# The first two gate tiles of a mixer kernel: weight units in other homes, the seventh product's weights and the third operand's sum made ahead, the third product in the second's bank

## The chip, the cores and the metric

The kernel runs on one core of a Trainium2 chip, as one launch. The metric is the device time of one execution in microseconds (us), the median of several runs. The core has five queues of instructions that run side by side and wait for one another by semaphores. In the profile they are PE (the matrix engine; PEld is its weight load), DVE (elementwise work), ACT (activations and copies), POOL (here mostly an issuer of DMAs) and SP (issues DMAs only).

## The reference

One layer of a backbone runs on 640 tokens: 512 of a denoising step and 128 of a context prefix. Width is 1024. After a norm and a modulation, `h` goes through an input projection into four mixers a, b, c, d (short convolution, HGRN2, neighbourhood attention, chunked gMLP), each 256 wide. They are joined by gates, and this is the part that the change touches:

```
g_a, g_b, g_c, g_d = split(sigmoid(h @ w_gate + b_gate), 4)
merged = (g_a * (y_a @ w_br_a) + g_b * (y_b @ w_br_b)
          + g_c * (y_c @ w_br_c) + g_d * (y_d @ w_br_d))
return merged @ w_o, ...
```

`w_gate` is 1024 x 4096 and each `w_br` is 256 x 1024. After it come `w_o`, a residual, a second norm and a feed-forward part with a convolution. Everything is float32.

## The kernel before

**Precision.** A float32 matrix product is done as three passes of a reduced type: each operand is split into a high half (a copy rounded by ACT) and a low half (the operand less its high half, on DVE), and high x high, high x low and low x high are summed. So each new operand or weight costs an ACT copy and a DVE subtraction before PE can use it.

**The gate stage.** The 16 pairs of gate tiles, in the order of `PAIRS`, go through `g_pair0` (pair 0) and `g_pair` (pairs 1 to 15, and a closing call). A pair is 2 x 2 blocks of outputs and of inputs and is done with seven products in place of eight (a Strassen scheme). `gprod(o, p, i, first)` is product i of the gate weights with operand `gx["x"][i]`: 4 blocks x 3 passes = 12 matmuls of 128 x 320. `bprod` is the same product of the branch weights with `y`: 3 matmuls. The sums of products run in PSUM banks: `first=True` begins a bank anew, `False` adds to what it holds. So products 1, 6 and 7 share one bank, with an ACT copy of the partial sum taken between them; in `g_pair0` before, products 5 and 3 share bank `b2`.

**Weights.** A pair has three weight units A, B, C of 128 x 2560 and a small one Z, made from raw weights: A and C are raw blocks, B two sums S, and Z one sum. `g_a`/`g_al`, `g_b`, `g_c` and `g_zh`/`g_zl` make the high and low halves. Product 1 and 2 read A, 5 and 6 B, 7 Z, 4 and 3 C. `gunit` gives a unit its home: unit k = 3p + i lives in one of three rotating `wp` buffers, or, every fourth, in the region "B", which the attention uses until its last matmuls. The raw weights come by SP into three rotating `rp` buffers or the region "G" (`gp_load`). The sums of pairs 0 and 1 are not made on DVE: `up_a23` has POOL add them up in DRAM (`gsum`) by DMAs long before, and pairs 0 and 1 only load them.

**Operands.** Products 1, 2, 4 and 3 read quadrants of `h`. Operands 6, 5 and 7 are differences, made and split by the generator `g_operands` (`place`) into the regions F, X1 and X0. Operand 3 of all pairs is replaced by a sum t3, which `g_operands` adds up and `g_pair0` splits (`g_split(3, ...)`). The memory of t3 then holds S (`gx["S"]`): in pair 1 a POOL DMA brings it (`g_s01`).

**What sets the order.** The generators (`attn`, `g_operands`, `up_a23`) are advanced by `tick`, which each product calls with its estimated time; a generator waits by polling a flag in `R`. Until `g_all` sets `fixed[0]`, a planner places the instructions of each engine by readiness, and by program order among those that are ready. From then on the calls through `ovec`, `oact`, `opool` and `omm` stay in program order on their engines: an instruction that waits holds up all that were written after it on its engine. SP's loads are left to the planner. All pinned calls go through one line, so line 150 in the profile stands for most of the gate stage; it is read by tile names (`w`, `B`, `S` weights; `m`, `g` banks; `ga`, `gb`, `y` gate sums; D holds operand 7's source and then t3 and S; G holds y's sums).

**Lines.** `g_operands` is at 1019 to 1080, `gp_load` and `gunit` at 1133 to 1154, `g_s01` to `g_zl` at 1167 to 1207, `g_pair0` at 1269 to 1327, `g_pair` at 1329 to 1412, the sums in DRAM at 1616 to 1624.

## Time and profile before

| | |
|---|---|
| median of 3 runs | 1005.3 us (1005.0 to 1007.15) |
| the profiled execution: its own time, its span | 1005.73 us, 1003.8 us |
| PE, PEld busy | 987.3 us (98%), 934.4 us (93%) |
| DVE, ACT, POOL busy | 864.7 us (86%), 592.6 us (59%), 195.5 us (19%) |
| DMA, mean over the span | 224 GB/s |
| mean granted PE clock | 0.995 |

A row of a timeline reads: start in us from the span's beginning, duration, engine, line, operation, output tile <- input tiles, shape, count; in square brackets, how long the engine had been idle before it and what released it. Rows of equal kind that follow one another are merged. A row of a table by stretches reads: the stretch, its length, then PE, PEld, DVE, ACT and POOL busy in us with their instruction counts, the granted PE clock (1.00 is full speed), the busy share of the DMA engines, and GB/s. A matmul's end is modelled: in a full-speed stream one starts every 0.147 us though each is shown as 0.31.

### The profile page before, as it was taken

What the parts mean: (1) busy time and instruction counts of PE and PEld (TensorE: products, weight loads), DVE (VectorE), ACT (ScalarE), POOL (GpSimd) and SP (SyncE); (2) the same over time, 40 slices, a digit from 0 to 9 for tenths busy, and PEclk for the clock granted to TensorE, in tenths of its full rate; (3) what the DMA queues carried; (4) which work ended last, traced back from release to release, by engine and by line L of the source; (5) the groups of instructions that cost most, each with busy time, mean ns of one, the idle gap of its engine ahead of it and who ended that gap; (6) DMA issues with size and microseconds to landing.
All of it is one profiled execution on the core that took longest, in us unless ns stands there. A gap on an engine that the chain in (4) does not pass through costs nothing.

```text
span 1003.8 us, 18999 instructions
## 1 busy us (share of the span) xinstructions
PE 987.3 (98%) x7437; PEld 934.4 (93%) x7437; DVE 864.7 (86%) x1413; ACT 592.6 (59%) x1034; POOL 195.5 (19%) x267
## 2 busy tenths in 40 slices
PE   8999999999979999999999999999999999999997
PEld 7899999999979999999998899999999999888886
DVE  6679899879878789898877778999999998999796
ACT  6652343445565655655655376777777777756672
POOL 1000022324023122243210021222222222100004
PEclk9999999999999999999999999999999999999999
DMA  9886349698169699999948775766666666976842
GB/s 354 333 292 246 113 149 257 175 283 241 54 222 252 179 261 315 222 313 269 260 123 351 280 283 173 226 154 173 174 166 168 176 170 192 347 261 217 300 131 105
DMA packets 75769, 224.92 MB, mean 224 GB/s; under 512 B 10432, under 2 KB 25312, under 8 KB 72992
## 3 DMA queue, kind: packets, MB, share of 16 engines
q1 hardware_dynamic: 44400, 149.25, 42.2%
q0 software_dynamic: 31280, 74.46, 31.6%
q8 instruction: 58, 0.95, 0.4%
q14 instruction: 31, 0.25, 0.1%
HBM read 182.64 MB, written 59.39 MB: 241 GB/s over the span
## 4 chain that ended last, share of the span: by engine, by line
PE 90%; DVE 5%; DMA 2%; issue 1%; POOL 1%; ACT 1%; SPq 0%; POOLq 0%; DVEq 0%; ACTq 0%
PE m L150 23%; PE g L1721 21%; PE g L374 11%; PE m L2184 8%; PE m L1721 5%; PE g L150 5%; PE m L1474 4%; PE g L2184 4%; PE g L955 2%; PE g L1474 1%; PE m L539 1%; PE m L1716 1%; DMA A<-in_w_ada_dram 1%; POOL hss L317 1%; PE m L955 1%
## 5 line engine op out<-in xcount | busy, mean ns | idle before, releaser
L374 PE MATMUL g<-XH,w 128*128 128x320 f32 x576 | 140.6, 318 | 0.0
L374 PEld LDWEIGHTS g<-XH,w 128*128 128x128 f32 x576 | 98.7, 188 | 2.4 <-issue 1.2
L150 PE MATMUL m<-XH,w 128*128 128x320 f32 x416 | 98.4, 311 | 1.7 <-DVE gb L150 1.7
L374 PE MATMUL g<-XL,w 128*128 128x320 f32 x288 | 89.0, 309 | 0.0
L150 PEld LDWEIGHTS m<-XH,w 128*128 128x128 f32 x416 | 70.8, 188 | 3.5 <-ACT ga L150 2.1
L150 PE MATMUL m<-XL,w 128*128 128x320 f32 x208 | 63.0, 310 | 0.0
L2184 PE MATMUL m<-w,XH 128*128 128x512 f32 x246 | 58.7, 390 | 0.0
L2184 PEld LDWEIGHTS m<-w,XH 128*128 128x128 f32 x246 | 46.1, 188 | 9.5
L374 PEld LDWEIGHTS g<-XL,w 128*128 128x128 f32 x288 | 54.2, 188 | 0.1
L150 DVE TENSOR_TENSOR w<-raw,w 128x640 fp32r<-128x640 f32 (+3 forms) x47 | 48.5, 1048 | 2.6 <-ACT w L150 2.6
L150 ACT ACTIVATE w<-raw 128x640 fp32r<-128x640 f32 (+3 forms) x53 | 48.5, 931 | 1.7 <-DMA raw<-in_w_in_dram 1.1
L150 POOL DMA_DIRECT2D wsum<-in_w_dn_dram x36 | 37.3, 1239 | 47.9 <-issue 31.4
L150 ACT ACTIVATE gb<-m 128x320 f32<-128x320 f32 x32 | 14.0, 437 | 49.0 <-PE m L150 49.0
L150 DVE SCALAR_TENSOR_TENSOR X<-MG,p2t,X 128x641 f32<-128x641 f32 x44 | 38.9, 884 | 1.0 <-ACT X L150 0.2
L150 DVE SCALAR_TENSOR_TENSOR X<-X,p2t,X 128x641 f32<-128x641 f32 x44 | 38.9, 884 | 0.9
L150 PEld LDWEIGHTS m<-XL,w 128*128 128x128 f32 x208 | 38.6, 188 | 0.6 <-issue 0.6
L1721 PE MATMUL g<-XL,w 128*128 128x320 f32 x240 | 38.6, 310 | 0.0
L1721 PE MATMUL g<-XL,C 128*128 128x320 f32 x240 | 38.3, 309 | 0.0
L1721 PEld LDWEIGHTS g<-XL,w 128*128 128x128 f32 x240 | 36.0, 188 | 0.6 <-ACT MG L150 0.3
L1721 PEld LDWEIGHTS g<-XL,C 128*128 128x128 f32 x240 | 36.0, 188 | 0.0
L150 PE MATMUL m<-X,S 128*128 128x320 f32 x192 | 32.3, 318 | 1.9 <-DVE S L150 1.9
L150 PE MATMUL m<-XH,B 128*128 128x320 f32 x128 | 31.9, 318 | 1.8 <-ACT m L150 1.8
(624 smaller groups left out, 2923.5 us busy)
## 6 DMA issues: line engine op xcount, KB each, us to landing
wsum<-in_w_dn_dram POOLq DMA_DIRECT2D x30, 512.0 KB, 11.6
raw<-in_w_gp_dram SPq DMA_DIRECT2D x23, 640.0 KB, 7.0
raw<-in_w_up_dram SPq DMA_DIRECT2D x28, 512.0 KB, 5.3
raw<-in_w_in_dram SPq DMA_DIRECT2D x19, 512.0 KB, 4.6
H<-in_w_adt_dram SPq DMA_DIRECT2D x19, 512.0 KB, 4.3
G<-in_w_up_dram SPq DMA_DIRECT2D x12, 512.0 KB, 5.1
raw<-wsum SPq DMA_DIRECT2D x12, 512.0 KB, 6.4
actx<-X POOLq DMA_DIRECT2D x22, 256.0 KB, 4.6
```

The costliest lines, as they stand in the source:

```text
L150: r = f(*args, **kw)
L317: pool.tensor_tensor(out, out, neghalf[:, 0:n], ALU.pow)
L374: mm(o, w[:, h, k0 + k, :], r(k)[:, s], start=(k == 0 and i == 0), stop=(k == kt - 1 and i == 2))
L539: mm(m[W * g:W * g + W, (i - s0) * W:(i - s0 + 1) * W], lhs, rhs, start=True, stop=True, tile_position=(64 * par, W * g))
L955: mm(o, x(kx)[:, ts], w[:, h, k, :], start=(kx == 0 and i == 0), stop=(kx == 7 and i == 2))
L1474: mm(m, mh[MHN[q]][:, hx, k % 2, t * P:(t + 1) * P], wo[q][:, hw, k % 2, :], start=(k == 0 and i == 0), stop=(k == 7 and i == 2))
L1716: mm(o, w[:, k, :], x[:, k, :], start=(first and not part and k == 0 and j == 0), stop=(part == 1 and k == 3), skip_group_check=True)
L1721: z = mm(o, w[:, k, :], x[:, k, :], start=(first and k == 0 and j == 0), stop=(k == 3 and j == 2), skip_group_check=True)
L2184: mm(ps, s[t // 4][:, hx, k, o:o + P], w[:, hw, k, c0:c1], start=first, stop=i == 2 and bi == len(batch) - 1 and k == len(ks) - 1, skip_gr ...
```

## The change

- `gunit`: the region "B" now takes the units with k mod 4 = 2 (was 3). Unit C of pair 0 lives there, unit A of pair 1 in a `wp` buffer, and so on in turn.
- `gsum` grows from two pairs to three: POOL makes the sums of pair 2 as well (18 DMAs in place of 12), and pair 2 loads its S by a POOL DMA and its third sum by SP, in place of three additions on DVE.
- `gp_load`: all loads go by SP. Pairs 0 and odd pairs use two `rp` buffers, other even pairs one and the region "G" (was the other way round). Pair 1's second block is no longer loaded by POOL from within pair 0; pair 2's load is issued inside pair 0.
- `g_operands`: unit B of pair 0 is cast as soon as the tile `ab0` is done, without waiting for `ab1`; then operands 6 and 5, t3, and both halves of Z. Unit C is cast after the attention's last part (`yc`), then operand 7.
- `g_pair0`: product 4 comes after products 1 and 2; t3's split and the load of S for pair 1 come between products 4 and 6; pair 1's unit A is cast before product 5; `gb` takes product 5 off right after it; product 3 begins bank `b3` (the second product's) anew, and is added to `gb` in an operation of its own. Units B, C and Z of pair 1 are no longer made here.
- `g_pair(1)`: units B, C, and the high half of Z are cast after the copy of product 1's branch part, and the low halves of Z and C after product 2 is issued. Pair 2's S load is issued behind them, and its second sum (`g_s23`) after product 5.

```diff
--- before.py
+++ after.py
@@ -1051,32 +1051,30 @@
         g_s23(0, r)
         while "ab0" not in R:
             yield 0.5
-        lows = g_c(0, r)
-        low(*lows[0])
-        while "ab1" not in R:
-            yield 0.5
         b = gw[0, "B"] = gunit(0, 1)
-        for i in range(2):
-            oact(b[:, 0, 1 - i], s[1 - i], AF.Copy)
-        low(b[:, 1, 1], s[1], b[:, 0, 1])
+        for i in (1, 0):
+            oact(b[:, 0, i], s[i], AF.Copy)
+            low(b[:, 1, i], s[i], b[:, 0, i])
         while "scores" not in R:
             yield 0.5
         place(6, a11, "F")
+        yield 0.5
+        place(5, a22, "X1")
         R["gx3"] = True
-        yield 1
-        place(5, a22, "X1")
-        low(b[:, 1, 0], s[0], b[:, 0, 0])
         yield 0.5
         ovec.tensor_tensor(a22, a12, a11, ALU.add)
-        g_zh(0, r)
-        gx["t3"] = a22
         gx["S"] = a22.rearrange("p a t -> p (a t)").rearrange("p (i k c) -> p i k c", i=2, k=5)
         gx["Y"] = a11.rearrange("p a t -> p (a t)")
         y_load(0)
-        low(*lows[1])
+        g_zh(0, r)
+        g_zl(0, r)
+        gx["t3"] = a22
         while "yc" not in R:
             yield 0.5
+        lows = g_c(0, r)
+        low(*lows[0])
         place(7, a21, "X0")
+        low(*lows[1])
         gx["Y1"] = a21.rearrange("p a t -> p (a t)")
 
     def g_split(i, x):
@@ -1124,7 +1122,8 @@
     def gp_id(p_):
         return PAIRS[p_]
 
-    gsum = dram.tile([2, P, 3, 5, P], F32, name="gsum")
+    GSUM = 3
+    gsum = dram.tile([GSUM, P, 3, 5, P], F32, name="gsum")
 
     def gp_raw(p_, h):
         bi, n = gp_id(p_)
@@ -1134,22 +1133,18 @@
 
         r = [rp.tile([P, 2, 5, P], F32, tag="raw", name=nm("raw"))]
         nc.sync.dma_start(r[0], gp_raw(p_, 0))
-        if p_ != 1:
-            gp_load2(p_, r)
-        return r
-
-    def gp_load2(p_, r):
-        r.append(region("G", [P, 2, 5, P]) if p_ % 2 else rp.tile([P, 2, 5, P], F32, tag="raw", name=nm("raw")))
-        if p_ > 1:
+        r.append(rp.tile([P, 2, 5, P], F32, tag="raw", name=nm("raw")) if p_ % 2 or not p_
+                 else region("G", [P, 2, 5, P]))
+        if p_ >= GSUM:
             nc.sync.dma_start(r[1], gp_raw(p_, 1))
         else:
-            eng = opool if p_ else nc.sync
-            eng.dma_start(r[1][:, 0], gp_raw(p_, 1)[:, 0])
-            eng.dma_start(r[1][:, 1], gsum[p_][:, 2])
+            nc.sync.dma_start(r[1][:, 0], gp_raw(p_, 1)[:, 0])
+            nc.sync.dma_start(r[1][:, 1], gsum[p_][:, 2])
+        return r
 
     def gunit(p_, i):
         k = 3 * p_ + i
-        if k % 4 == 3:
+        if k % 4 == 2:
             return region("B", [P, 2, 2, 5, P], F32R)
         return wp.tile([P, 2, 2, 5, P], F32R, tag="w", name=nm("w"))
 
@@ -1167,8 +1162,8 @@
     def g_s01(p_, r):
 
         s = gw[p_, "S"] = [gx["S"][:, i] for i in range(2)]
-        if p_ == 1:
-            opool.dma_start(gx["S"], gsum[1][:, 0:2])
+        if p_ < GSUM:
+            opool.dma_start(gx["S"], gsum[p_][:, 0:2])
             return
         ovec.tensor_tensor(s[0], r[0][:, 0], r[1][:, 1], ALU.add)
         ovec.tensor_tensor(s[1], s[0], r[1][:, 0], ALU.add)
@@ -1176,7 +1171,7 @@
     def g_s23(p_, r):
         s = gw[p_, "S"]
         b21, (b22, b12) = r[0][:, 1], (r[1][:, 0], r[1][:, 1])
-        if p_ > 1:
+        if p_ >= GSUM:
             ovec.tensor_tensor(b12, b12, b22, ALU.add)
         ovec.tensor_tensor(b21, s[1], b21, ALU.add)
 
@@ -1279,51 +1274,43 @@
         oact(ga[:, 0:HC], b1, AF.Copy)
         bprod(p1_, 0, 1, True)
         oact(p3_, p1_, AF.Copy)
-        gprod(b4, 0, 4, True)
         gprod(b3, 0, 2, True)
         ovec.tensor_tensor(ga[:, 0:HC], b3, ga[:, 0:HC], ALU.add)
         g_sig(0, 0, ga[:, 0:HC], ga[:, 0:HC])
         bprod(p3_, 0, 2, False)
+        drain(lambda: "Y1" in gx)
+        gprod(b4, 0, 4, True)
+        g_split(3, gx["t3"])
+        g_s01(1, r[1])
         gprod(b1, 0, 6, False)
         oact(gb[:, 0:HC], b1, AF.Copy)
-        drain(lambda: "t3" in gx)
-        g_split(3, gx["t3"])
-        g_s01(1, r[1])
-        drain(lambda: "Y1" in gx)
+        g_a(1, r[1])
+        y_sums()
         gprod(b2, 0, 5, True)
-        g_zl(0, r[0])
-        g_a(1, r[1])
+        ovec.tensor_tensor(gb[:, 0:HC], b2, gb[:, 0:HC], ALU.subtract)
+        gx["C"] = region("MG1", [P, 2, 3, HC], F32R)
+        lows, x3 = y_split()
+        oact(x3[2], x3[1], AF.Copy)
         gprod(b1, 0, 7, False)
         oact(gb[:, HC:T], b1, AF.Copy)
-        y_sums()
+        for x in lows + [x3]:
+            low(*x)
         ovec.tensor_tensor(ga[:, HC:T], b4, gb[:, HC:T], ALU.add)
         g_sig(0, 0, ga[:, HC:T], ga[:, HC:T])
         ovec.tensor_tensor(gb[:, HC:T], b2, gb[:, HC:T], ALU.subtract)
-        gx["C"] = region("MG1", [P, 2, 3, HC], F32R)
-        lows, x3 = y_split()
-        oact(x3[2], x3[1], AF.Copy)
-        for x in lows + [x3]:
-            low(*x)
-        gp_load2(1, r[1])
+        r[2] = gp_load(2)
+        gprod(b3, 0, 3, True)
         g_al(1, r[1])
-        gprod(b2, 0, 3, False)
         y = gw[0, "y"] = gp.tile([P, T], F32, tag="gt", name=nm("y"))
         c2_ = gw[0, "b2"] = pm()[:, 0:HC]
         bprod(p1_, 0, 6, False)
         oact(y[:, 0:HC], p1_, AF.Copy)
+        ovec.tensor_tensor(gb[:, 0:HC], b3, gb[:, 0:HC], ALU.add)
         bprod(c2_, 0, 5, True)
-        ovec.tensor_tensor(gb[:, 0:HC], b2, gb[:, 0:HC], ALU.subtract)
         bprod(p1_, 0, 7, False)
         oact(y[:, HC:T], p1_, AF.Copy)
         ovec.tensor_tensor(y[:, HC:T], c2_, y[:, HC:T], ALU.subtract)
-        late = []
-        g_b(1, late)
         g_s23(1, r[1])
-        late += g_c(1, r[1])
-        r[2] = gp_load(2)
-        g_zh(1, r[1])
-        for x in late:
-            low(*x)
         gx["Y"] = gx["Y1"]
 
     def g_pair(p_, r):
@@ -1345,7 +1332,8 @@
         b1, b3 = pm()[:, 0:HC], pm()[:, 0:HC]
         ga = gw[p_, "gt", 0] = gp.tile([P, T], F32, tag="gt", name=nm("ga"))
         gb = gw[p_, "gt", 1] = gp.tile([P, T], F32, tag="gt", name=nm("gb"))
-        g_zl(p_, r[p_])
+        if q:
+            g_zl(p_, r[p_])
         gprod(b1, p_, 1, True)
         g_sig(q, 1, gw[q, "gt", 1], gw[q, "gt", 1])
         oact(b3, b1, AF.Copy)
@@ -1354,23 +1342,36 @@
         p1_, p3_ = ps[:, 1, 0:HC], ps[:, 0, 0:HC]
         bprod(p1_, p_, 1, True)
         oact(p3_, p1_, AF.Copy)
+        if not q:
+            g_b(p_)
+            late = g_c(p_, r[p_])
+            g_zh(p_, r[p_])
         g_merges(q)
         if nx:
             g_a(n, r[n])
+            if q:
+                g_s01(n, r[n])
+        gprod(b3, p_, 2, False)
+        if not q:
+            g_zl(p_, r[p_])
+            for x in late:
+                low(*x)
             g_s01(n, r[n])
-        gprod(b3, p_, 2, False)
         lows, x3 = y_split() if new else ([], None)
         g_sig(p_, 0, ga[:, 0:HC], b3)
         for x in lows:
             low(*x)
         if nx:
             g_al(n, r[n])
-            g_s23(n, r[n])
+            if q:
+                g_s23(n, r[n])
         gprod(b1, p_, 6, False)
         oact(gb[:, 0:HC], b1, AF.Copy)
         bprod(p3_, p_, 2, False)
         b2 = pm()[:, 0:HC]
         gprod(b2, p_, 5, True)
+        if not q:
+            g_s23(n, r[n])
         if nx and not new:
             g_b(n)
         gprod(b1, p_, 7, False)
@@ -1616,12 +1617,13 @@
         while "stc" not in R:
             yield 1
         for o, h, i, add in ((0, 0, 0, 0), (2, 1, 0, 0), (0, 1, 1, 1), (2, 1, 1, 1), (1, None, 0, 0), (1, 1, 0, 1)):
-            for p_ in range(2):
+            for p_ in range(GSUM):
                 bi, n = gp_id(p_)
                 g = gsum[p_][:, i] if h is None else gp_raw(p_, h)[:, i]
                 z = pool.dma_start(gsum[p_][:, o], g, accum_op=ALU.add) if add else pool.dma_start(gsum[p_][:, o], g)
                 tc.keep_in_program_order(z)
-                yield 0.7
+                if p_ != 1:
+                    yield 0.5
 
     def up_early():
         x = region("XH", [P, 5, 8, P])
```

## The prediction

> **What bounds the kernel now.** The page first: PE is busy 98% of the span, and the chain that ended last is PE for 90%. A table by stretches of 100 us has PE busy throughout in most of them (the row shown is after the gate stage).
>
> ```profile
> PE 90%; DVE 5%; DMA 2%; issue 1%; POOL 1%; ACT 1%; SPq 0%; POOLq 0%; DVEq 0%; ACTq 0%
> 700.00:800.00 100.00, 100.00 (x684) 100.00 (x683) 94.78 (x146) 71.72 (x124) 24.53 (x32) 1.00 0.63 169
> ```
>
> So a change on another engine counts only where PE waits. The grouped list of PE's waits has its three longest, one instruction each, in the gate stage. PE's timeline gives their places:
>
> ```profile
> 274.46 0.41 PE L150 MATMUL m<-XH,w 128*128 128x320 f32 x1
> ...
> 284.44 0.46 PE L150 MATMUL m<-X,S 128*128 128x320 f32 x2
> 286.80 3.00 PE L150 MATMUL m<-X,S 128*128 128x320 f32 x10 [1.90 <-DVE S L150]
> 291.53 0.39 PE L150 MATMUL m<-XH,w 128*128 128x320 f32 x1 [1.74 <-DVE gb L150]
> ...
> 297.75 0.60 PE L150 MATMUL g<-E,B 128*128 128x320 f32 x3
> 300.19 0.41 PE L150 MATMUL m<-XH,B 128*128 128x320 f32 x1 [1.84 <-ACT m L150]
> ...
> 305.34 0.60 PE L150 MATMUL g<-E,B 128*128 128x320 f32 x3
> 305.78 1.92 PE L150 MATMUL m<-X,w 128*128 128x320 f32 x12
> ...
> 314.00 0.46 PE L150 MATMUL m<-XH,w 128*128 128x320 f32 x2
> ```
>
> Three matmuls take 305.78 - 305.34 = 0.44 us, 0.1467 each; twelve take 1.76. Pair 0 starts at 274.46, pair 2 with the second matmul of the last row, at 314.15: 39.69 us for 204 matmuls (14 gate products of 12, 12 branch products of 3), which need 204 x 0.1467 = 29.92. Lost: 9.77 us. Product 7 starts at 284.44, so product 3 was due at 284.44 + 1.76 = 286.20 and starts at 291.53: 5.33. Pair 1's product 2 was due at 297.75 + 0.44 = 298.19 and starts at 300.19: 2.00. The 24 matmuls after it take 305.34 - 300.19 = 5.15 in place of 3.52: 1.63. The other 0.81 are small waits. The table by stretches shows why those matmuls are slow:
>
> ```profile
> 283.20:286.60 3.40, 1.70 (x12) 1.44 (x10) 2.09 (x2) 2.44 (x3) 0.29 (x1) 1.00 0.26 105
> 286.60:290.00 3.40, 3.00 (x10) 2.60 (x10) 2.02 (x5) 0.17 (x1) 0.24 (x1) 0.54 0.60 173
> 290.00:293.40 3.40, 1.87 (x13) 1.90 (x14) 2.34 (x5) 2.18 (x5) 0.00 (x0) 0.96 0.53 212
> 296.90:300.30 3.40, 1.56 (x11) 1.30 (x11) 3.40 (x5) 3.21 (x7) 2.29 (x4) 1.00 0.91 255
> 300.30:303.70 3.40, 3.40 (x14) 3.40 (x15) 3.27 (x6) 1.50 (x3) 2.47 (x4) 0.53 1.03 300
> ```
>
> Two stretches with PE busy for 1.70 and 1.56 of 3.40 us were each followed by one at half clock (0.54, 0.53); the one with 1.87 was not. I read from this that a stretch less than about half busy costs the next its clock. The Trainium skill, "TensorE: Matmul & The Clock Gate" (Part 1: The HAM clock gate), says that the clock falls to half after a whole idle window of some 3.4 us, and gives as rule to have no idle gap above that. By the rule the gaps here would cost no clock, and the sum below would be 1.63 + 1.37 = 3.0 us smaller; the trace decides against it.
>
> **Part 1, product 7 (wait for S).** These rows say why it waited:
>
> ```profile
> 273.76 1.37 ACT L150 ACTIVATE w<-s 128x640 fp32r<-128x640 f32 x2 [2.98 <-PE g L374]
> 275.19 1.26 ACT L676 ACTIVATE A<-MG 128x1280 fp32r<-128x1280 f32 x1
> 278.43 1.26 ACT L150 ACTIVATE X<-D 128x1280 fp32r<-128x1280 f32 x1
> 279.59 0.42 ACT L150 ACTIVATE ga<-m 128x320 f32<-128x320 f32 x1
> 279.90 0.43 ACT L150 ACTIVATE g<-g 128x320 f32<-128x320 f32 x1
> 284.51 1.49 DVE L150 TENSOR_TENSOR XL<-D,XH 128x1280 fp32r<-128x1280 f32 x1 [2.82 <-ACT XH L150]
> 285.92 0.82 DVE L150 TENSOR_TENSOR S<-raw,S 128x640 fp32r<-128x640 f32 x1
> 273.76 0.82 DVE L435 TENSOR_TENSOR MG<-g,MG 128x640 f32<-128x640 f32 x1 [2.66 <-PE g L374]
> ```
>
> Z's low half stood on DVE behind operand 3's (284.51), which waited for ACT. In the change t3's sum (1.49) and Z's halves (0.74, 0.82) are written while tile `ab1` runs, and the hole is there: before 273.76 DVE had been idle for 2.66 us and ACT for 2.98. It fits nearly (1.49 + 0.82 = 2.3), so I put the wait at nothing; if it does not fit, the last 0.8 to 2.3 us land on the chain of the next paragraph. Operand 3's split gets product 6, 5 and 7 (5.3 us) as cover. With the wait goes the half clock: the 10 matmuls took 3.00 in place of 1.63, 1.37 of the 5.33.
>
> **What is late next, (a).** Unit C of pair 0 now lives where the attention reads until 274.5, so its two copies (0.64 each from start to start) come after that, where B's were. On ACT from 274.57: attention's own copy 0.16, C 1.28, operand 7's high half 1.16, A<-MG 1.16, then `ga`'s copy 0.31, and the copy that the second branch product waits for ends 0.43 later, at 279.07; PE follows at 279.13. As product 4 no longer lies between, PE is there after 274.46 + 1.76 + 0.44 + 1.76 and 0.1 of small waits, at 278.53. Loss 0.60; nothing if the planner takes `ga` first, 2 more if Z's or t3's work lands here. C's low half needs 0.82 after 275.4 and product 4 comes at 279.6: covered.
>
> **Part 2, product 3 (wait for gb).** Its bank was the one that `gb` still had to be taken from. Bank `b3`'s last reader (`ga`, at 281.2 before) is long done, so this wait is gone: 5.33 - 2.07 - 1.37 = 1.89. The operation added on DVE (0.49) lies beside products 5 and 7. The next thing due is pair 1's unit A, at about 290.0 by PE. What DVE has to do before it:
>
> ```profile
> 292.05 1.23 DVE L150 TENSOR_TENSOR MG<-G,MG 128x640 fp32r<-128x640 f32 x2 [0.66 <-ACT MG L150]
> 293.19 0.49 DVE L150 TENSOR_TENSOR E<-G,E 128x320 fp32r<-128x320 f32 x1
> ```
>
> The lows of y (1.23 + 0.49), a `ga` and a `gb` operation (0.49 each) and A's low half (1.49, as XL above), 4.2 from 286.0, when y's sums are copied: 290.2, for the third matmul at 290.3. Just covered; each 0.5 that DVE is late would show.
>
> **Part 3, pair 1's product 2 (wait for m).** ACT made four casts and a sigmoid, from 295.65 on, in front of the copy at 299.72:
>
> ```profile
> 295.65 1.26 ACT L150 ACTIVATE w<-D 128x1280 fp32r<-128x1280 f32 x1
> 299.72 0.41 ACT L150 ACTIVATE m<-m 128x320 f32<-128x320 f32 x1
> 296.95 1.49 DVE L150 TENSOR_TENSOR w<-D,w 128x1280 fp32r<-128x1280 f32 x1
> ```
>
> Now the casts come behind both copies, so 2.00 and 1.63 go. But **(b)** product 6 needs B's low half, which was ready early. With pair 1 starting at 289.99, its branch product 1 starts at 289.99 + 1.76 + 0.88 = 292.63; the copy starts 0.64 later (a product's length and the latency, 0.60 + 0.04), B's high half 0.34 after that at 293.61, the low half 1.30 later (295.65 to 296.95) and ends 1.49 on, at 296.40. Product 6's third matmul was due at 293.07 + 1.76 + 0.29 = 295.12 and comes at 296.46. Loss 1.34; by the spread of the start, 0.9 to 1.8. Z's and C's lows and the merges follow on DVE (6 x 0.8) and meet products 7 and 4 at 300 and 303: covered.
>
> **(c), pair 2's S.** It was made by DVE; now it is a POOL DMA that must wait until pair 1's B is cast, as they share memory. Behind it wait ACT's copy of S, and behind that the copy of `gb` that product 4 needs.
>
> ```profile
> 286.31 0.54 POOL L150 DMA_DIRECT2D D<-gsum  x1 [9.80 <-DVE XL L150]
> D<-gsum POOLq DMA_DIRECT2D x1, 640.0 KB, 5.3
> D<-A POOLq DMA_DIRECT2D x1, 640.0 KB, 11.1
> D<-A SPq DMA_DIRECT2D x1, 640.0 KB, 3.6
> G<-in_w_gp_dram SPq DMA_DIRECT2D x1, 640.0 KB, 12.5
> ```
>
> The same load for pair 1 was issued 0.31 after its release and landed in 5.3. So: 296.40 + 0.31 + 5.3 = 302.01, ACT 1.20, the copy 0.44 and 0.06 to PE: 303.71. PE arrives at 296.46 + 1.47 + 0.44 + 1.76 + 1.76 + 0.88 = 302.77. Loss 0.94; nothing at 3.6 to land, 8.1 at 12.5. I take 5.3, the same transfer, since the five POOL DMAs of the weights' later sums that stood in the queue at 295 to 298 (DMA share 0.91 and 1.03 above) are now issued behind pair 1's S, by 287.
>
> **The rest costs nothing.** The six added DMAs lengthen POOL's chain of sums:
>
> ```profile
> 148.18 2.17 POOL L1622 DMA_DIRECT2D gsum<-in_w_gp_dram  x4
> 187.09 1.05 POOL L317 TENSOR_TENSOR hss<-hss,neghalf 128x4 f32<-128x4 f32 x1 [14.68 <-DVE hss L316]
> ```
>
> It ran from 148.18 to 187.09 - 14.68 = 172.41. Half as much again ends at 184.5, inside the 14.68 us that POOL was idle; without that cover the mixer's root at 187 would be late, and by no more than the 12.1 added. Three additions (0.82 each, as S above) leave DVE for pair 2. SP's extra loads wait for buffers freed about 10 us before their use. The homes turn by the same step of four. A steady pair has no PE wait in the list above.
>
> **The sum.** 9.77 lost before; left are the small waits 0.81, (a) 0.60, (b) 1.34, (c) 0.94 = 3.69. Gain 6.1 us, which nothing behind gives back where PE is never idle, as in the row at 700. The profiled execution took 1005.73: 999.6. The median of the runs is 0.4 lower, so 999.2.
>
> **Rivals.**
> 1. *No new waits.* ACT takes `ga` first, S lands in under 4.4 us, and (b) shrinks to nothing. All of 8.96 is gained: 1005.3 - 8.96 = 996.3. For it: 3.6 for a transfer of this size; against it: B's two steps in a row on ACT and DVE.
> 2. *The weights are not ahead.* t3 and Z miss the hole, as the attention's last softmax work stands in it. Then 2.3 us return at (a), and with 0.60 that is 2.9 idle in one stretch, so about 1.5 of half clock: 999.2 + 3.8 = 1003.0. For it: ACT and DVE order is by readiness there; against it: both were idle.
> 3. *Slower: pair 2's S lands late.* At 12.5 us, the slowest landing of its size, (c) becomes 8.1 and half a clock stretch adds 1.6: 999.2 + 7.2 + 1.6 = 1008.0. It decides against the change from 5.3 + 6.1 - 1.6 = 9.8 us to land. For it: 11.1 and 12.5 were seen within 5 us of that place; against it: they were among twice the traffic, and the same load took 5.3. The Trainium skill, "SBUF — State Buffer" (SBUF: two separate sides), tells of a way to this: a DMA issued from POOL can stand still while DVE holds the port they share. In this trace the load that took 5.3 was issued (286.31) while DVE's row of 285.92 still ran, which speaks against it.
>
> **Chances.** Forecast 0.63 (997.5 to 1001.5), no new waits 0.15, not ahead 0.10, late S 0.09, else 0.03. A measurement here tells 0.2%, 2.0 us, from no change, so faster is below 1003.3. The first two and two thirds of the third lie there: 0.85. The rest of the third and a third of the late S are the same, 0.07 with what is else; slower 0.08. The range takes in rival 1 and rival 2 and leaves out the late S: 996.0 to 1003.8.
>
> **What would show it.** Right: no PE wait for S or gb; pair 2 starts near 308; the copies of m and g in pair 1 start within 0.1 us of their product; PE waits about 1 us each for ACT's `g`, DVE's B and ACT's `gb`; the granted clock stays at 1.00 from 284 to 308. Wrong: a half clock stretch there, a POOL `D<-gsum` that lands after 302.8, or PE waits between 150 and 200.

## The result, and the profile after

The changed kernel takes 998.83 us (median; 997.91 to 999.27) against 1005.98 for the kernel before beside it (1005.0 to 1007.15). The ratio is 0.9927, with a 95% interval of 0.9910 to 0.9944: about 7.3 us faster. The profiled execution took 999.27 us with a span of 997.5; before it was 1005.73 and 1003.8, so its span fell by 6.3. The forecast was 999.2, faster. Below, TensorE is the profile's PE, VectorE its DVE, ScalarE its ACT, GpSimd its POOL and SyncE its SP.

The first view is TensorE's timeline of the changed kernel (start, length, engine, line, operation, operands, count, and in brackets the idle time before it with what ended it), with the rows that answer those shown of before.

```profile
276.35 0.60 PE L150 MATMUL g<-E,w 128*128 128x320 f32 x3
278.94 0.70 PE L150 MATMUL g<-E,w 128*128 128x320 f32 x3 [0.23 <-ACT g L150]
...
284.76 1.92 PE L150 MATMUL m<-X,S 128*128 128x320 f32 x12
286.52 0.31 PE L150 MATMUL m<-XH,B 128*128 128x320 f32 x1
...
294.98 0.56 PE L150 MATMUL m<-F,w 128*128 128x320 f32 x2
296.51 1.73 PE L150 MATMUL m<-F,w 128*128 128x320 f32 x10 [0.97 <-DVE w L150]
...
308.65 0.60 PE L150 MATMUL g<-E,w 128*128 128x320 f32 x3
```

Product 7 (284.76) runs as one group of twelve, and product 3 (286.52) follows it directly: the waits for `S` and for `gb` are gone, and so is the one for `m` in pair 1. Two waits are new: 0.23 us for ScalarE's `g` and 0.97 for unit B's low half. The gate stage is measured below from pair 0's first branch product (276.35, before 276.33) to pair 2's (308.65), between which lie 204 matmuls: 32.30 us. The kernel before has its second mark here:

```profile
276.33 0.60 PE L150 MATMUL g<-E,w 128*128 128x320 f32 x3
...
315.90 0.60 PE L150 MATMUL g<-E,w 128*128 128x320 f32 x3
```

That is 39.57 us, so the two pairs gained 7.27 us. The table by stretches of the changed kernel (length, busy time of PE, PEld, DVE, ACT, POOL, then granted clock, DMA share, GB/s) shows no stretch at half clock:

```profile
283.40:286.80 3.40, 3.40 (x25) 3.40 (x24) 3.30 (x7) 2.73 (x5) 2.56 (x5) 1.00 0.97 332
286.80:290.20 3.40, 3.31 (x23) 3.00 (x21) 3.37 (x7) 1.50 (x5) 1.25 (x3) 1.00 1.00 417
293.60:297.00 3.40, 2.43 (x15) 1.98 (x15) 2.04 (x2) 3.40 (x6) 0.25 (x1) 1.00 1.09 298
297.00:300.40 3.40, 3.40 (x25) 3.40 (x24) 3.37 (x6) 1.77 (x3) 3.40 (x7) 1.00 0.91 267
...
440.00:450.00 10.00, 8.91 (x59) 8.39 (x58) 8.77 (x12) 5.92 (x10) 3.84 (x3) 1.00 1.06 302
```

The last row is the surprise. In pair 10, long behind the change, TensorE is idle for 1.09 us. The kernel before has no such gap in the gate stage's second half:

```profile
430.00:510.00 80.00, 80.00 (x548) 79.95 (x546) 72.39 (x97) 46.59 (x75) 25.18 (x28) 1.00 1.03 258
```

So 7.27 gained and 1.09 given back make 6.18, against the 6.3 of the span. Where the 1.09 come from is told by the rows of VectorE, GpSimd's and SyncE's queues and TensorE there:

```profile
414.99 0.33 SPq L1094 DMA_DIRECT2D D<-ycd  x1
422.13 0.90 POOL L150 DMA_DIRECT2D D<-ycd  x1 [4.59 <-DVE C L150]
432.32 2.07 DVE L150 TENSOR_TENSOR D<-D 128x320 f32<-128x320 f32 x4 [1.55 <-DMA D<-ycd]
442.26 0.42 PE L150 MATMUL m<-XH,w 128*128 128x320 f32 x1 [0.57 <-ACT gb L150]
445.24 0.42 PE L150 MATMUL m<-XH,w 128*128 128x320 f32 x1 [0.52 <-DVE gb L150]
```

The last branch's `y` is loaded in two steps, SyncE's high part and GpSimd's low part added on top. VectorE's sums over it waited 1.55 us for the second, and that delay reached TensorE as two waits, 0.57 + 0.52 = 1.09. In the kernel before the same sums came without a wait, just in time:

```profile
422.24 0.33 SPq L1096 DMA_DIRECT2D D<-ycd  x1
429.26 0.90 POOL L150 DMA_DIRECT2D D<-ycd  x1 [5.63 <-DVE C L150]
438.01 2.07 DVE L150 TENSOR_TENSOR D<-D 128x320 f32<-128x320 f32 x4
```

The second load decides it. The list of transfers (count, size, median us from issue to landing) has it so, first in the kernel before, then in the changed one:

```profile
D<-ycd POOLq DMA_DIRECT2D x1, 640.0 KB, 8.7
D<-ycd POOLq DMA_DIRECT2D x1, 640.0 KB, 10.2
```

Before, it landed at 429.26 + 8.7 = 437.96, some 0.05 us ahead of the sums. VectorE was ready for the sums 15.8 us after the first load was issued in both kernels (438.01 - 422.24 before, 432.32 - 1.55 - 414.99 after): the change moved the load and the need for it alike. What differs is that the second load took 1.5 us longer.

### The profile page after: what moved, and what is told of

It reads as the page before. It is cut to its first block, busy times and chain, and to the rows that moved or that the text cites. A ratio compares the mean times of both kernels' runs of the same rounds, so it can differ in the third digit from the quotient of the medians.

```text
span 997.5 us, 19012 instructions
## 1 busy us (share of the span) xinstructions
PE 984.5 (99%) x7437; PEld 931.6 (93%) x7437; DVE 861.9 (86%) x1411; ACT 592.5 (59%) x1034; POOL 199.9 (20%) x272
## 4 chain that ended last, share of the span: by engine, by line
PE 85%; DVE 6%; DMA 5%; issue 1%; ACT 1%; POOL 1%; SPq 0%; POOLq 0%; DVEq 0%
PE g L1723 21%; PE m L150 20%; PE m L2186 9%; PE g L374 9%; PE m L1723 5%; PE g L150 4%; PE m L1475 4%; PE g L2186 4%; PE g L955 2%; PE g L1475 1%; PE m L539 1%; DMA D<-hdr 1%; PE m L1718 1%; DMA D<-ycd 1%; DMA ybd<-D 1%
## 5 line engine op out<-in xcount | busy, mean ns | idle before, releaser
L150 ACT ACTIVATE X<-X,p2t 128x641 f32<-128x641 f32 x22 | 20.4, 927 | 18.4 <-DVE X L150 18.4
L150 ACT ACTIVATE X<-g 128x320 f32<-128x320 f32 x30 | 13.1, 437 | 30.6 <-PE g L1723 30.6
```

Of the source, the lines that this page charges most:

```text
L150: r = f(*args, **kw)
```

## The experiments

Three questions: do the three parts each give what the sum put down to them; what are the waits that are left worth; and who gives back in pair 10. All times are medians, and ratios are to the kernel before on the same chip, with their 95% intervals. The runs come from more than one chip and session, in which the kernel before had medians from 1005.25 to 1006.95; its row below belongs to the changed kernel's first row, and other rows are compared by their ratios or as said. "Pairs 0+1" is the distance defined above, "pair 10" TensorE's busy time from 440 to 450 us, both in the profiled execution.

```
kernel                             us       ratio (95%)              pairs 0+1  pair 10
before                             1005.98  1                        39.57     10.00
changed                             998.83  0.9927 (0.9910, 0.9944)  32.30       8.91
changed, second time                999.43  0.9925 (0.9913, 0.9937)  33.38       9.48
+ y first                           998.80  0.9919 (0.9906, 0.9932)  32.71      10.00
+ halves of B                       999.33  0.9924 (0.9911, 0.9938)  32.90       9.37
+ y first, halves of B              998.62  0.9922 (0.9909, 0.9934)  32.76      10.00
+ B of pair 2 behind the copies     998.17  0.9931 (0.9918, 0.9945)  32.29      10.00
+ all three                         996.77  0.9913 (0.9900, 0.9925)  31.08      10.00
- third product's bank             1001.78  0.9963 (0.9950, 0.9977)  35.98      10.00
- sums of pair 2                   1000.86  0.9956 (0.9945, 0.9968)  34.24       9.64
before + Z's low half             1004.51  0.9989 (0.9980, 0.9999)  38.39      10.00
before + bank                     1004.44  0.9990 (0.9979, 1.0002)  38.12      10.00
before + casts                    1006.60  1.0008 (0.9994, 1.0021)  38.06       8.04
before + casts, y first           1004.72  0.9985 (0.9972, 0.9997)  38.06      10.00
```

### The parts alone, on the kernel before

**Z's low half alone.**

```diff
         g_zh(0, r)
+        g_zl(0, r)
         gx["t3"] = a22
...
         gprod(b2, 0, 5, True)
-        g_zl(0, r[0])
```

> On the kernel before, one line moved: Z's low half is taken right behind its high half, ahead of the gate stage. Expected: product 7's wait for S (1.90, with the step 2.07 us) and its ten matmuls at half clock (1.37) go, so product 3 is due at 286.2. Its bank is free only when gb has been taken from it; VectorE's y sums (2.06 from 285.9), ga and gb (0.49 each) come first, so at about 288.9: the wait for gb is 2.7 us in place of 1.89. Product 3 then starts 2.6 us earlier than the 291.53 of before. Theory (a stretch of 3.4 us less than half busy costs the next its clock): some 1.4 us of half clock return and the gain is about 1.2 us, 1005.7. Rival (only a gap as long as the stretch costs the clock): the granted clock stays at 1.00 from 284 to 296 and the gain is 2.6 us, 1004.4.

Measured: 0.9989, 1.1 us faster; pairs 0+1 1.18 us shorter. TensorE's timeline of this kernel, and two of its stretches:

```profile
285.00 1.92 PE L150 MATMUL m<-X,S 128*128 128x320 f32 x12
289.71 0.38 PE L150 MATMUL m<-XH,w 128*128 128x320 f32 x1 [2.79 <-DVE gb L150]
```

```profile
286.80:290.20 3.40, 0.61 (x4) 0.52 (x4) 2.56 (x6) 1.63 (x4) 0.54 (x1) 1.00 0.57 188
290.20:293.60 3.40, 3.40 (x17) 3.34 (x15) 3.38 (x5) 1.08 (x3) 1.45 (x3) 0.59 0.13 30
```

The wait for `S` is gone; the wait for `gb` grew from 1.74 to 2.79, and a stretch at clock 0.59 follows it. The part moves most of its gain into the next wait and the stretch behind it. The clock and the gain are those of the first theory (1.2 us).

**The bank alone.**

```diff
+        ovec.tensor_tensor(gb[:, 0:HC], b2, gb[:, 0:HC], ALU.subtract)
         ovec.tensor_tensor(ga[:, HC:T], b4, gb[:, HC:T], ALU.add)
...
-        gprod(b2, 0, 3, False)
+        gprod(b3, 0, 3, True)
...
-        ovec.tensor_tensor(gb[:, 0:HC], b2, gb[:, 0:HC], ALU.subtract)
+        ovec.tensor_tensor(gb[:, 0:HC], b3, gb[:, 0:HC], ALU.add)
```

> On the kernel before, only product 3 goes into the other bank. Expected: product 7 still waits 1.90 us for S and runs at half clock, and product 3 follows it without a wait, 1.9 us earlier, at 289.65. Theory of the parts' sum: the gain is those 1.9 us, 1005.1. Rival (the chain behind ga sets the end there): pair 1's unit A is ready no earlier than before, since VectorE's and ScalarE's work for it hangs on product 7 and not on product 3; its low half ended at 295.0 and pair 1 would now be due at 293.2, so TensorE waits there for about 1.5 us and only 0.4 us is gained, 1006.5.

Measured: 0.9990, not told from no change; pairs 0+1 1.45 us shorter. TensorE's timeline of this kernel:

```profile
287.22 1.73 PE L150 MATMUL m<-X,S 128*128 128x320 f32 x10 [1.90 <-DVE S L150]
291.23 0.42 PE L150 MATMUL g<-MG,w 128*128 128x320 f32 x1 [0.52 <-ACT MG L150]
292.09 0.56 PE L150 MATMUL g<-MG,w 128*128 128x320 f32 x2 [0.44 <-DVE MG L150]
```

The wait for `gb` is gone, but the branch product behind it now waits for y's splits (0.52 and 0.44, and 0.15 more a little later): they hang on `ga`, which hangs on product 7. And the ten matmuls of product 7 take 1.73 us here, behind the same wait of 1.90 us after which they took 3.00 in the kernel before. That is 1.27 of the 1.45, and not put down to the bank, since the casts alone show the same full clock behind the same wait; what the bank gives alone is then about 0.2, near the rival's 0.4, though the wait is for y's splits and not for unit A.

**The casts alone, and with y first.**

```diff
-        late = []
-        g_b(1, late)
         g_s23(1, r[1])
-        late += g_c(1, r[1])
         r[2] = gp_load(2)
-        g_zh(1, r[1])
-        for x in late:
-            low(*x)
...     (in g_pair, for pair 1, behind the copies of m and g)
+            g_b(p_)
+            late = g_c(p_, r[p_])
+            g_zh(p_, r[p_])
...     (behind the issue of product 2)
+            g_zl(p_, r[p_])
+            for x in late:
+                low(*x)
             g_s01(n, r[n])     (now behind these; in later pairs still ahead of product 2)
```

> On the kernel before, only pair 1's casts go behind the two copies. Expected: the wait for m (1.84, with the step 2.00 us) and the half clock behind it (1.63) go, and product 6 waits for B's low half (1.24 in the changed kernel): gain 2.0 + 1.63 - 1.24 = 2.4 us, 1004.6. If the half clock has another cause than that wait, the granted clock around 300 stays below 1.00 and the gain is 0.8 us, 1006.2.

Measured: 1.0008, no gain at all, although pairs 0+1 are 1.51 us shorter and the clock is 1.00 from 297 on. Of the 1.51 again 1.27 is product 7 at full clock, so the edit gave 0.24 there in place of 2.4. TensorE's timeline shows what took the rest:

```profile
300.67 1.73 PE L150 MATMUL m<-F,w 128*128 128x320 f32 x10 [0.97 <-DVE w L150]
...
308.15 0.42 PE L150 MATMUL m<-XH,w 128*128 128x320 f32 x1 [0.91 <-ACT gb L150]
...
311.14 0.42 PE L150 MATMUL m<-XH,w 128*128 128x320 f32 x1 [0.52 <-DVE gb L150]
```

The first wait was expected, (b). The two others are new: here VectorE makes pair 2's `S`, behind the casts' low halves, and the copy of `gb` and the subtraction behind it are late. And then the time went in pair 10. VectorE's and TensorE's timelines there, and the stretch:

```profile
439.84 2.07 DVE L150 TENSOR_TENSOR D<-D 128x320 f32<-128x320 f32 x4 [2.94 <-DMA D<-ycd]
...
449.77 0.41 PE L150 MATMUL m<-XH,w 128*128 128x320 f32 x1 [1.96 <-ACT gb L150]
```

```profile
440.00:450.00 10.00, 8.04 (x55) 7.77 (x54) 9.69 (x14) 3.94 (x6) 1.90 (x3) 1.00 1.09 344
```

The load of the last branch landed 2.94 us too late and took 1.96 us from TensorE here, and 0.53 a little later. To see whether that is the whole of it, the same kernel once more, with the load of the last branch ahead of five transfers for the down weights in GpSimd's queue:

```diff
         for p_ in range(1, GPAIR + 1):
+            if p_ == 9:
+                y_load(3)
             for _ in range(5):
                 next(sums_, None)
...     (and no longer in g_pair(9))
```

> The kernel before with pair 1's casts behind the copies, as in the run that came out 0.1% slower than before although pair 2 started 1.5 us earlier, and now with the last branch's second load ahead of pair 9's sums too. Theory (its gain was given back in pair 10, where TensorE was busy for 8.04 of 10 us behind a load that took 11.5 us to land): the load lands in about 8.6, the stretch from 440 is busy throughout, and the ratio falls from 1.0008 by 1.5 to 2.0 us to 0.999. Rival (the loss is elsewhere): it stays at 1.0008.

VectorE's timeline and the stretch:

```profile
436.78 2.06 DVE L150 TENSOR_TENSOR D<-D 128x320 f32<-128x320 f32 x4
```

```profile
440.00:450.00 10.00, 10.00 (x71) 10.00 (x70) 9.79 (x13) 5.97 (x9) 5.10 (x6) 1.00 1.19 241
```

Measured: 0.9985 where it was 1.0008, 2.3 us less, with the same 38.06 us in pairs 0+1. VectorE waits for nothing, and pair 10 is busy throughout: the load is what took the time there. The theory said 1.5 to 2.0. The size is less sure than the mechanism, for the executions of the casts alone differ widely: six of the twelve show a mean granted clock of 0.992 to 0.995 and take 1006.21 to 1010.00 us, the six others, at 0.997 or more, take 1003.49 to 1006.98. With y first only two of eleven are at such a low clock (1007.21 and 1007.49), and the rest take 1003.69 to 1005.29. Where the others lost their clock is not on record, since the one profiled lost none in these stages.

### One part undone in the changed kernel

```diff
-        ovec.tensor_tensor(gb[:, 0:HC], b2, gb[:, 0:HC], ALU.subtract)
         gx["C"] = region("MG1", [P, 2, 3, HC], F32R)
...
-        gprod(b3, 0, 3, True)
+        gprod(b2, 0, 3, False)
...
-        ovec.tensor_tensor(gb[:, 0:HC], b3, gb[:, 0:HC], ALU.add)
+        ovec.tensor_tensor(gb[:, 0:HC], b2, gb[:, 0:HC], ALU.subtract)
```

> On the changed kernel, only product 3 goes back to the bank it had before. Expected: it waits until gb has been taken from that bank, which VectorE does right behind ga (in the changed kernel ga at 287.79, the next operation at 288.31 for 0.49), so about 2.4 us from 286.5 on. Theory (a stretch less than half busy costs the next its clock): a stretch of half clock follows, 1.4 us more: 999.4 + 3.8 = 1003.2. Rival (only a gap as long as a stretch costs it): clock 1.00, 999.4 + 2.4 = 1001.8. If the sum that stood for this part in the prediction (1.89 us, and no clock) is the whole of it: 1001.3.

Measured: 1001.78, 0.9963, which is 0.0038 or 3.8 us above the changed kernel's 0.9925, but 2.4 to 3.0 above its two medians. Pairs 0+1 take 35.98 us, 2.6 to 3.7 more. TensorE's timeline and a stretch:

```profile
289.37 0.41 PE L150 MATMUL m<-XH,B 128*128 128x320 f32 x1 [2.25 <-DVE gb L150]
```

```profile
286.80:290.20 3.40, 1.15 (x8) 0.88 (x7) 3.29 (x6) 1.46 (x4) 1.07 (x4) 1.00 1.01 416
290.20:293.60 3.40, 3.40 (x16) 3.27 (x15) 1.00 (x2) 0.44 (x1) 0.89 (x1) 0.53 1.03 381
```

The wait of 2.25 us came back, with a stretch at clock 0.53 behind it, as the first theory said and its rival did not. The time alone would not have told them apart: 1001.78 is the rival's 1001.8 and not the theory's 1003.2. Part of this is pair 10, which is busy throughout here, while the changed kernel gives back 0.5 to 1.1 us there. Alone the bank shortens pairs 0+1 by 0.2 us, as the last part on top of the others by 2.6 to 3.7. No run undoes Z's low half or the casts alone.

The second edit undone is the third pair of sums made in memory:

```diff
-    GSUM = 3
+    GSUM = 2
```

> On the changed kernel, only pairs 0 and 1 get their sums from memory, and pair 2's are VectorE's again. Theory (with the load of S the wait for it goes, but three additions of 0.82 us return to VectorE in pair 1, S being free only when unit B's low half and the other lows are done, at about 300.6 us): S is ready at 302.2, its cast at 303.5, so the copy of gb is as late as with a load that lands in 5.4 us; time as the changed kernel within 1 us. If the six added transfers cost something between 150 and 190 us, or the loads crowd pair 1, it is faster by that; if the additions push the late weights of product 7 or 4, slower by 0.8 to 2.4 us.

Measured: 1000.86, 0.9956: slower than the changed kernel by 1.4 us (medians) or 3.1 us (ratios). Pairs 0+1 take 34.24 us, 0.9 to 1.9 more. TensorE's timeline:

```profile
304.24 0.42 PE L150 MATMUL m<-XH,w 128*128 128x320 f32 x1 [0.90 <-ACT gb L150]
307.22 0.41 PE L150 MATMUL m<-XH,w 128*128 128x320 f32 x1 [0.52 <-DVE gb L150]
```

The casts alone show the same two waits (0.91 and 0.52), there too with pair 2's additions on VectorE. So the casts give their gain only with the third pair of sums in memory, which is worth 34.24 - 32.30 = 1.94 us here, or 0.86 against the changed kernel's second execution, whose load was late (below). The late copy of `gb` was expected (0.90); that the subtraction in front of product 3 is late too (0.52) was not, and "within 1 us" was missed. What else lies between that and the 3.1 of the ratios was not located.

### The waits that are left

The changed kernel once more, as the base:

> The changed kernel as it is, as the base of the next three: 998.8 us, 0.7% below the kernel before. Where its profile gave time back: at 440 to 450 us TensorE was busy for 8.91 of 10.00 us, waiting for gb in pair 10, and two pairs earlier VectorE's sums for the last branch had waited 1.55 us for their second load, which took 10.2 us to land. If that is a fixed property and no accident of one execution, the window shows about 8.9 here too.

Measured: 999.43, 0.9925. Pair 10 is busy for 9.48 us, so it gives back 0.52 here and 1.09 in the first execution. Another wait has come up instead, in ScalarE's and TensorE's timelines of this execution:

```profile
302.47 1.27 ACT L150 ACTIVATE w<-D 128x1280 fp32r<-128x1280 f32 x1 [3.50 <-PE m L150]
303.65 0.42 ACT L150 ACTIVATE gb<-m 128x320 f32<-128x320 f32 x1
...
304.12 0.41 PE L150 MATMUL m<-XH,w 128*128 128x320 f32 x1 [0.83 <-ACT gb L150]
```

with the load behind it in the list of transfers (count, size, median us to landing), first this execution's and then the first one's:

```profile
D<-gsum POOLq DMA_DIRECT2D x1, 640.0 KB, 5.4
```

```profile
D<-gsum POOLq DMA_DIRECT2D x1, 640.0 KB, 4.3
```

Pair 2's `S` landed after 5.4 us here and after 4.3 in the first execution. It was issued at 296.96 here, so it landed at 302.4, when the cast starts; the bracket of that row names TensorE, whose product 7 ends at about the same time. ScalarE's cast of it stands ahead of the copy that product 4 needs, and pairs 0+1 are 33.38 - 32.30 = 1.08 us longer.

**y first** on the changed kernel is the edit shown above.

> The last branch's second load is put ahead of pair 9's five sums of down weights in GpSimd's queue; since it waits there for the first load, those five start some 19 us later and leave the transfer engines to the two loads. Theory (the 1.09 us given back in pair 10 come from the late load): the two loads land in 4.4 to 6.6 us each, VectorE's sums wait for nothing, TensorE is busy for 10.0 of the 10 us from 440, and the time falls by about 1.1 us, to 997.7. Rival (the transfer engines are full whatever the order, or the wait for gb in pair 10 is VectorE's own load of work): the load lands no earlier than 432 us or the window keeps its 8.9, and the time stays at 998.8.

Measured: 998.80, 0.9919. The mechanism is the theory's: VectorE's sums at 431.01 wait for nothing and pair 10 is busy for 10.00. It is SyncE's load that gains, 4.0 us in place of 6.4; GpSimd's still takes 8.6, outside the 4.4 to 6.6 expected. The time is not the theory's 997.7 but the rival's 998.8: it differs from the changed kernel's second median by 0.6 us, which the intervals don't tell from nothing.

**Halves of B.**

```diff
-            g_b(p_)
+            b = gw[p_, "B"] = gunit(p_, 1)
+            for i in (1, 0):
+                oact(b[:, 0, i], gx["S"][:, i], AF.Copy)
+                low(b[:, 1, i], gx["S"][:, i], b[:, 0, i])
```

> In pair 1 unit B is rounded and its low part taken half by half, the half of product 6 first. Theory (product 6 waits only because both halves are done in one piece): its waits of 0.97 and 0.27 us, together 1.24, go, and the time falls by 1.0 to 1.2 us to about 997.7. Rival (VectorE is the bound of pair 1, 9.4 of 10 us busy): the wait moves to product 5 or 7 or to the late C weights, and the time stays at 998.8. A second rival: what is gained in pair 1 makes the loads of pair 9 late by as much more, and 998.8 stays though the wait is gone.

Measured: 999.33, 0.9924, no gain. TensorE's timeline:

```profile
297.52 1.92 PE L150 MATMUL m<-X,w 128*128 128x320 f32 x12
299.29 1.92 PE L150 MATMUL m<-X,S 128*128 128x320 f32 x12
303.65 0.41 PE L150 MATMUL m<-XH,w 128*128 128x320 f32 x1 [1.56 <-ACT gb L150]
```

Product 6's wait is gone and TensorE is 1.2 us earlier at product 7, and stands for 1.56 us at product 4: the load, 5.4 us again, did not come earlier by as much. None of the three cases expected names this place, though the sum's own term (c) does.

**Both.**

> Both edits. If the two are independent, 998.8 less 1.1 less 1.2 = 996.5 us. If the second rival of the halves is right (a gain ahead of pair 9 is given back there), the halves gain only where the load is early, so this one falls by the sum while the halves alone gain nothing.

Measured: 998.62, 0.9922. Pair 10 is busy throughout, and a wait of 1.42 us for `gb` at product 4 is what is left in pairs 0+1. The 996.5 of independent edits was missed.

**B of pair 2 behind the copies.** For that wait, only the order is changed: in pair 1 the unit's cast comes behind the copies of `gb` and `y`.

```diff
-        if nx and not new:
+        if nx and not new and q:
             g_b(n)
...
-        if new:
+        if new or not q:
             g_b(n)
```

> On the changed kernel, pair 2's unit B is cast behind the copies of gb and y in pair 1, so that no copy that TensorE needs stands behind the load of S. Theory (product 4 waits for gb only because that copy stands behind the cast in ScalarE's queue; 0.83, 0.15 and 0 us in three executions by a landing of 5.4, 4.8 and 4.4 us): the wait is 0 wherever the load lands, the next one for gb goes too, and product 6's wait of 0.97 us stays; from pair 0's first branch product to pair 2's it takes 32.3 us, as in the best of the earlier executions. The time falls by 0 to 1 us, and perhaps nothing of it is left behind pair 9, where the load of the last branch is late. Rival (the wait is VectorE's): the wait stays, at its low half of unit B.

Measured: 998.17, 0.9931: no wait for `gb` in pairs 0+1, 32.29 us there, and no gain to be told in the time. The load landed in 4.6 us in this execution, so it shows little by itself. A sixth execution took 1947.34 us, for a reason that its record does not show; the median is that of the five others. Pair 10 is busy for 10.00 here although the load of the last branch was not moved: its second part landed after 8.8 us.

**All three.**

> The three edits on the changed kernel: the last branch's load ahead of the sums, unit B of pair 1 in halves, pair 2's unit B behind the copies. If the three waits are the whole of what is still lost, pair 0's first branch product to pair 2's takes 32.3 - 1.24 = 31.1 us, the stretch 440 to 450 is busy throughout, and the time is 2.0 to 3.0 us below the changed kernel's, a ratio to the kernel before of 0.990 in place of 0.9925. Rival: a further wait takes their place, at 0.992.

Measured: 996.77 (996.57 to 997.56), 0.9913. TensorE's and ScalarE's timelines and the load:

```profile
276.18 0.60 PE L150 MATMUL g<-E,w 128*128 128x320 f32 x3
...
307.26 0.60 PE L150 MATMUL g<-E,w 128*128 128x320 f32 x3
...
300.86 0.44 ACT L150 ACTIVATE gb<-m 128x320 f32<-128x320 f32 x1 [2.23 <-PE m L150]
301.30 0.44 ACT L150 ACTIVATE y<-g 128x320 f32<-128x320 f32 x1
301.63 1.26 ACT L150 ACTIVATE w<-D 128x1280 fp32r<-128x1280 f32 x1
```

The load took 5.4 us, and the copy at 300.86 ran without waiting for it: this execution shows what the one before could not. Pairs 0+1 take 31.08 us, as worked out (31.1). It is the fastest kernel of the study, below the lowest of the nine runs of the changed kernel (997.91) in all four of its runs; by medians it is 2.7 us faster than the 999.43 on the same chip, by ratios 1.2 us, and the two intervals overlap, so its size is open.

## Why the prediction was right, and where not

The time was right to 0.4 us, but that is in part luck: two steps erred, in opposite directions and by about the same size.

- *What is removed* held: the waits for `S`, `gb` and `m` are gone and the clock is 1.00 throughout. Taken apart, though, the sum's terms do not stand by themselves. Pairs 0+1 shrink by 1.18, 1.45 and 1.51 us with the parts alone, together 4.14, and by 7.27 with the whole. Against a kernel before with product 7 at full clock (39.57 - 1.27 = 38.30, an estimate) the parts give -0.09, 0.18 and 0.24, together 0.3, and the whole 6.0. The 1.89 for the bank measured 0.2 alone and 2.6 to 3.7 as the last. The sum could add them only because the change takes them all, the third pair of sums among them, which the sum had at nothing and which measured 0.9 to 1.9.
- *The half clock of 1.37 at product 7* was put down to the wait for `S`. Three other executions with the same wait of 1.90 us (bank alone, casts alone, casts with y first) ran product 7 at full clock. (Its size is 3.00 - 1.73 = 1.27 by these rows.) It belongs to the execution profiled as much as to the kernel. The other executions of the kernel before say the same: of thirty on one chip, four with a mean granted clock of 0.999 took 1002.60 to 1003.67 us and four at 0.993 took 1006.72 to 1007.99, while all nine of the changed kernel are at 0.998 or 0.999, at 997.91 to 1000.37. So of the 7.3 us some 3 are lost clock that the kernel before does not meet every time (an estimate, from the middle of the four fastest, 1002.9, and of the nine, 999.0, not all on the same chip).
- *(a), the copy of g*, 0.60: the products came at 278.55 by the pace of the first, and ran at 278.94, 0.39. Right in kind, a third too large.
- *(b), unit B's low half*, 1.34: the third matmul ran at 296.51 in place of 294.98 + 0.29, 1.24. Right. But what it costs is not what its removal gives: without it product 4 waits for the load instead.
- *(c), pair 2's S*, 0.94 from a landing of 5.3 us: 0 in the first execution (4.3), 0.83 of wait in the second (5.4). The mechanism is shown: the load, ScalarE's queue, product 4. The landing is not one number.
- *"Which nothing behind gives back"* is the step that failed. The prediction named rows that are busy throughout as the reason, but a busy row does not say how much slack its loads have. The last branch's second load had some 0.05 us before, with 8.7 to land. In the changed kernel it took 10.2, and 1.09 us went back; in the casts alone 11.5, and 1.96 and 0.53. It is not the shorter stage that does it: the need comes 15.8 us after the first load's issue before, in the changed kernel and in the casts alone, and with B of pair 2 behind the copies, where it does too, the stage is as short (32.29), the load took 8.8 and TensorE lost nothing. With (a), (b) and (c) too large by 0.21 + 0.10 + 0.94 = 1.25, the two errors cancel.
- *The rivals*: no new waits (996.3) is what the kernel with all three edits comes to, 996.8, by taking away waits that the change has. The weights were ahead, and the load was never late by more than a wait of 1.56.
- *The 12.1 added to GpSimd's chain of sums* hid as expected: TensorE is busy for 99.90 of the 100 us from 100 to 200, before 99.89.

```profile
100.00:200.00 100.00, 99.90 (x1535) 95.11 (x1535) 91.69 (x187) 39.79 (x87) 26.19 (x32) 1.00 0.66 195
```

## What to carry to other kernels

Waits in a chain are not worth their length one by one: removing one can hand most of its time to the next, and one removed last can seem to give it all, as the bank did. So test parts both alone and as the one undone. Where an engine is busy without a break, ask of each transfer how much earlier than needed it lands: a load with no slack costs nothing in one execution and a microsecond in the next. And look at what stands in a queue behind an instruction that waits for a transfer; here moving that instruction behind two copies cost nothing, and the copies ran on time with the load at 5.4 us.

## What was not expected of the hardware

- The clock halved behind idle gaps shorter than the 3.4 us of a stretch: after 2.25 us (0.53) and 2.79 us (0.59), and each time after 1.81 to 1.84 us at pair 1's product 2 (0.53 before, 0.51 with the bank alone, 0.54 with Z's low half alone). After 1.90 us at product 7 it halved in one execution and not in three others, and after 1.74 us in none of the three that had it. That a stretch less than half busy costs the next its clock fits these, but not every such stretch did: in the casts alone the wait of 1.96 us in pair 10 left TensorE busy for 1.44 of the 3.40 us from 446.6, and the clock of the next stretch is 1.00. Where a stretch begins was not to be seen, and it is left open what decides between 1.7 and 2.0. The Trainium skill, "TensorE: Matmul & The Clock Gate" (Part 1: The HAM clock gate), has the clock fall after a whole idle window of some 3.4 us; no gap here was that long, so the runs differ from it.
- The same accumulating load of 640 KB, issued by GpSimd, landed after 8.3 to 11.5 us in pair 9, with a DMA share of 1.13 to 1.17 from 415 to 436 us in the four executions read there. With five other transfers held back the first load took 3.9 to 4.0 us in place of 6.4 to 6.9, and the second stayed at 8.1 to 8.6. Among the ten executions with the old order, the landing goes with how long before the load GpSimd issued the latter of two transfers for the down weights: 8.3 to 8.8 us where that was 7.3 to 7.8 us earlier, 8.7 to 9.7 where it was 6.1 to 6.9, 10.2 at 5.8 (the changed kernel, 416.31 to 422.13) and 11.5 at 5.1 (the casts alone). No run moves those two alone, so this is not shown to be the cause, and why they come later in some executions was not found.
